# A transformer trunk on one core: the passage into the FFN with its order written out anew

## The chip, the cores and the metric

One core of one Trainium2 chip runs the whole program. The time is device microseconds of one execution. The kernel before: 1216.84, 1217.25 and 1219.11 us, median 1217.25.

## The reference

One layer of a hybrid trunk on 1024 tokens of width 1024: a modulated RMSNorm, one input projection, a Mamba-2 group and a chunked attention group side by side, an output projection, and then the FFN, which is the part that matters here:

```python
h = rmsnorm(x, norm_ffn_w[l]) * (1 + sc_f) + sh_f
x = x + gate_f * conv_ffn(h, w_up, ffn_conv_w, w_down)

def conv_ffn(h, w_up, conv_w, w_down):
    u = causal_dwconv(h @ w_up, conv_w)      # 3 taps, causal
    g, val = jnp.split(u, 2, axis=-1)
    return (jax.nn.silu(g) * val) @ w_down   # 1024 -> 2 x 2816 -> 1024
```

All of it is float32.

## The kernel before

**Engines.** TensorE (PE) multiplies, VectorE (DVE) and ScalarE (ACT) do elementwise work and read the products out of PSUM, GpSimd (POOL) does a little, SyncE (SP) issues loads.

**Float32 by splitting.** Each operand is split into a high and a low half: `split` (L80) lets ScalarE write the rounded high half, and then VectorE the rest, source minus high. `mm3` (L75) makes three matmuls of it: high by high, high by low, low by high. In the third the stationary or moving part is the low half, so a product can begin with the high half of its weights alone.

**Seven products.** The up product h @ w_up is done in the Strassen-Winograd form, seven products of half-size blocks for each of 22 column tiles ("units"). The table `PRODS` (L1070) lists for each product the weight row, the input and the PSUM tile: P1 and P2 go to uX, Q6, Q7 and Q4 to uY, Q5 and P3 to uZ. Each of these adds up in its bank, and after each product `post` (L1103) reads the running value out: P1 to `cv` and P2 to `cg` (ScalarE copies), Q6 to `cg`, Q7 and Q4 to `cv` (VectorE subtractions), P3 to `cg`. Q7 has a second subtraction, of uZ as Q5 left it, before P3 adds onto the same uZ. The subtractions are what frees the bank for the next product that adds to it.

**Units in pairs.** Units i and 11 + i are taken together, eleven pairs. Weight rows come from DRAM into `ya` and `xs` (rows 0 to 3, L1076 and L1077; the next pair is loaded when these rows have been read), `sums` (L1079) makes rows 4 to 7 from them, `prep` (L1086) splits two rows at once into a ring tile `w` of 128x1024 high and as much low, and `prep_s4` (L1242) splits row 7 of both units for P3. The ring of five places (`HOMES`, L1044: places 0 to 2 are buffers of earlier stages, 3 and 4 the buffers r12 and r22 that first hold the raw inputs b12 and b22) gives a place in the order of the two tables FIRST and AGAIN. A place is free when the products with its weights are done, or its first contents have been read.

**Inputs.** The seven inputs b11, b21, t1 to t4 and b22 are made of h once: blocks of h turned by TensorE into `xps`, scaled into the raw buffers (`a`, `rt`, `rb` in the profile), added and subtracted on VectorE, and split: `b11h/b11l`, `b21h/b21l`, `t1h/t1l`, `tH/tL` (t2 and t3 in the first pair of tiles, t4 and b22 in the second). `h_last` (L1218) splits one of the last four, in two halves of 128x1024.

**The passage.** L1193 to L1250 is the stage in which the inputs are finished while the first pair's products already run. Here the engines V, A and T are wrapped in `InOrder` (L45): with `on` set, each instruction is issued behind the one before it in the text. Elsewhere a scheduler with a cost model sets each engine's order. The profile shows rows of the wrapped instructions as L58. Behind the passage the loop (L1328) does what is left of the first pair, then ten more pairs, and the convolution (`conv`, L1127: one ScalarE row `a<-cv`, two VectorE rows), the gate and the stores to DRAM. The last pair's gate is done in the down product, which follows.

## Time and profile before

| | us |
|---|---|
| median of three executions | 1217.25 |
| the profiled execution | 1217.67 |
| its span | 1215.9 |
| TensorE busy | 1162.3 |
| VectorE busy | 942.3 |
| ScalarE busy | 594.9 |

All times within the run are microseconds from the start of the span. The passage begins near 551, the second pair of units at 611.53, the down product after 990. In the rows of the engines a name stands for a tile without its number: `w<-xs` is a weight split of the second unit, `w<-ya` one of the first.

### The profile page before, as it was taken

What the parts mean: (1) busy time and instruction counts of PE and PEld (TensorE: products, weight loads), DVE (VectorE), ACT (ScalarE), POOL (GpSimd) and SP (SyncE); (2) the same over time, 40 slices, a digit from 0 to 9 for tenths busy, and PEclk for the clock granted to TensorE, in tenths of its full rate; (3) what the DMA queues carried; (4) which work ended last, traced back from release to release, by engine and by line L of the source; (5) the groups of instructions that cost most, each with busy time, mean ns of one, the idle gap of its engine ahead of it and who ended that gap; (6) DMA issues with size and microseconds to landing.
All of it is one profiled execution on the core that took longest, in us unless ns stands there. A gap on an engine that the chain in (4) does not pass through costs nothing.

```text
span 1215.9 us, 15656 instructions
## 1 busy us (share of the span) xinstructions
PE 1162.3 (96%) x5802; PEld 976.8 (80%) x5802; DVE 942.3 (77%) x1413; ACT 594.9 (49%) x1001; POOL 195.2 (16%) x174
## 2 busy tenths in 40 slices
PE   5999999999999989999899999999999999999995
PEld 4887888778889978888688888888888888888884
DVE  7756455598697788747899988988889779766976
ACT  4637465663333657676454543444434445433443
POOL 1109373782210134200000000000000000000002
PEclk9999999999999999999999999999999999999998
DMA  9632121323554301141223223322333278733533
GB/s 355 237 94 83 36 74 39 129 81 127 174 174 157 104 18 36 61 147 53 70 80 129 96 104 130 118 81 87 105 130 112 91 265 293 261 118 125 169 117 138
DMA packets 56683, 151.91 MB, mean 125 GB/s; under 512 B 5664, under 2 KB 5792, under 8 KB 55200
## 3 DMA queue, kind: packets, MB, share of 16 engines
q1 hardware_dynamic: 49552, 126.54, 31.3%
q10 hardware_dynamic: 7056, 24.38, 5.0%
q8 instruction: 45, 0.74, 0.3%
q14 instruction: 30, 0.25, 0.1%
HBM read 117.61 MB, written 29.10 MB: 121 GB/s over the span
## 4 chain that ended last, share of the span: by engine, by line
PE 67%; DVE 7%; ACT 2%; DMA 1%; issue 1%; POOL 0%; DVEq 0%; POOLq 0%; SPq 0%; ACTq 0%
PE dn L76 6%; PE dn L77 6%; PE dn L78 6%; PE wops L702 6%; PE uY L76 5%; PE uY L78 5%; PE uY L77 5%; PE uZ L78 3%; PE uZ L77 3%; PE uZ L76 3%; PE uX L78 3%; PE uX L77 3%; PE uX L76 3%; PE s L76 2%; PE s L77 2%; PE s L78 2%
## 5 line engine op out<-in xcount | busy, mean ns | idle before, releaser
L978 POOL TENSOR_TENSOR st<-st,mhalf 128x1 f32<-128x1 f32 x16 | 12.7, 799 | 691.7 <-DVE st L977 680.3
L76 PE MATMUL dn<-w 128*128 128x512 f32 x308 | 111.9, 389 | 0.0
L77 PE MATMUL dn<-w 128*128 128x512 f32 x308 | 111.9, 389 | 0.0
L78 PE MATMUL dn<-w 128*128 128x512 f32 x308 | 103.3, 389 | 0.0
L76 PE MATMUL uY<-tH,w 128*128 128x512 f32 x256 | 99.7, 390 | 1.8 <-ACT w L58 1.8
L410 POOL TENSOR_SCALAR p<-p,st 128x640 f32<-128x640 f32 (+4 forms) x64 | 98.5, 1554 | 13.6 <-DVE st L409 10.4
L78 PE MATMUL uY<-tH,w 128*128 128x512 f32 x256 | 99.6, 389 | 0.0
L77 PE MATMUL uY<-tL,w 128*128 128x512 f32 x256 | 99.6, 389 | 0.0
L85 ACT ACTIVATE w<-ya 128x1024 fp32r<-128x1024 f32 (+1 forms) x41 | 39.1, 955 | 86.1 <-PE uY L78 80.8
L702 PE MATMUL wops<-hH,yhl 128*128 128x512 f32 x224 | 74.9, 403 | 2.6 <-ACT yhl L85 1.4
L78 PEld LDWEIGHTS dn<-w 128*128 128x128 f32 x308 | 57.8, 188 | 12.1
L76 PEld LDWEIGHTS dn<-w 128*128 128x128 f32 x308 | 57.8, 188 | 12.0
L77 PEld LDWEIGHTS dn<-w 128*128 128x128 f32 x308 | 57.8, 188 | 11.9
L85 ACT ACTIVATE pt<-tp 128x512 fp32r<-128x512 f32 (+2 forms) x72 | 36.6, 523 | 48.6 <-PE tp L436 19.7
L404 DVE CUSTOM_DVE_ANT_0 p<-s,bias 128x640 f32<-128x640 f32 (+4 forms) x64 | 40.6, 650 | 25.4 <-PE tp L439 8.5
L86 DVE TENSOR_TENSOR pt<-tp,pt 128x512 fp32r<-128x512 f32 (+2 forms) x72 | 41.9, 595 | 22.3 <-ACT pt L85 13.4
L76 PEld LDWEIGHTS uY<-tH,w 128*128 128x128 f32 x256 | 48.0, 188 | 12.1 <-ACT w L58 2.2
L77 PEld LDWEIGHTS uY<-tL,w 128*128 128x128 f32 x256 | 48.1, 188 | 10.0
L78 PEld LDWEIGHTS uY<-tH,w 128*128 128x128 f32 x256 | 48.1, 188 | 9.9
L85 ACT ACTIVATE w<-xs 128x1024 fp32r<-128x1024 f32 (+1 forms) x41 | 38.9, 952 | 32.4 <-PE uY L78 32.4
L702 PEld LDWEIGHTS wops<-hH,yhl 128*128 128x128 f32 x224 | 42.4, 191 | 11.9 <-ACT yhl L85 1.7
L76 PE MATMUL s<-hH,wh 128*128 128x512 f32 x128 | 50.6, 395 | 0.9 <-DVE ct L515 0.9
(472 smaller groups left out, 3426.8 us busy)
## 6 DMA issues: line engine op xcount, KB each, us to landing
gz<-a ACTq DMA_DIRECT2D x10, 1024.0 KB, 5.3
wos<-in_w_ada_dram SPq DMA_DIRECT2D x18, 512.0 KB, 4.1
ya<-in_w_up_dram SPq DMA_DIRECT2D x11, 768.0 KB, 4.2
xs<-in_w_up_dram SPq DMA_DIRECT2D x11, 768.0 KB, 4.4
adat<-in_w_ada_dram SPq DMA_DIRECT2D x16, 512.0 KB, 6.4
raws<-in_w_ft_dram SPq DMA_DIRECT2D x16, 512.0 KB, 3.6
qk<-in_w_ada_dram SPq DMA_DIRECT2D x14, 512.0 KB, 4.4
gy<-a ACTq DMA_DIRECT2D x10, 512.0 KB, 2.6
```

The source lines that it names most:

```text
L76: T.matmul(ps, lh, rh, start=start, stop=False, skip_group_check=more)
L77: T.matmul(ps, lh, rl, start=False, stop=False, skip_group_check=more)
L78: T.matmul(ps, ll, rh, start=False, stop=stop, skip_group_check=more)
L85: i = A.activation(hi, src, AF.Copy) if ehi is A else ehi.tensor_copy(hi, src)
L86: return i, elo.tensor_tensor(lo, src, f32(hi), ALU.subtract)
L404: V.tensor_tensor_reduce(out=dst, in0=src, in1=bsl, scale=-1.0, scalar=3e38, op0=ALU.add, op1=ALU.min, accum_out=nm)
L410: G.tensor_scalar(pv_, pv_, rr, None, op0=ALU.mult)
L702: i = op(*a, **k)
L978: G.tensor_tensor(r, ms, mhalf[:, 0:1], ALU.pow)
```

## The change

In the passage the text, and so the order on each engine, becomes: the second unit's split for Q5 and Q6 stands ahead of the split of t2 and ahead of the copy of P2 to `cg`. For this `product` gets a switch that leaves the copy out, and `post` is called on its own. The sums for row 6 and the first unit's split for Q7 and Q4 stand ahead of the split of t3, the second unit's behind it. The seventh products (Q7) move from the loop into the passage, the first between the two halves of t4's split, the second behind row 7's sums; the second subtraction of Q7 becomes `minus_z` and ends the passage. The split of the last weights (row 7) is put between the halves of b22's split. The ring gives the seventh tile (these last weights) place 2 instead of 4, and the turn after it runs 0, 4, 1, 3, 2 instead of 2, 0, 1, 3, 4. No arithmetic is added or left out.

```diff
-    FIRST, AGAIN = (0, 1, 2, 0, 1, 3, 4), (2, 0, 1, 3, 4)
+    FIRST, AGAIN = (0, 1, 2, 0, 1, 3, 2), (0, 4, 1, 3, 2)
...
-        def product(self, p):
+        def product(self, p, post=True, z=True):
...
-            self.post(p, ps)
+            if post:
+                self.post(p)
+            if z and p == "Q7":
+                self.minus_z()
...
             elif p == "Q7":
                 V.tensor_tensor(self.v[:, 512:S], ps, self.v[:, 0:512], ALU.subtract)
-                V.tensor_tensor(self.v[:, 512:S], self.v[:, 512:S], self.ps["Z"], ALU.subtract)
...
+        def minus_z(self):
+            V.tensor_tensor(self.v[:, 512:S], self.v[:, 512:S], self.ps["Z"], ALU.subtract)
...
-    h_last("t2", "t2")
-    u0.product("P2")
-    u1.prep("Q5", "Q6")
+    u0.product("P2", post=False)
+    u1.prep("Q5", "Q6")
+    h_last("t2", "t2")
+    u0.post("P2")
     u1.product("P2")
...
     for u in units:
         u.product("Q5")
-    h_last("t3", "b12")
     for u in units:
         u.sums((6,))
-    for u in units:
-        u.prep("Q7", "Q4")
-    for u in units:
-        u.product("Q6")
-    h_last("t4", "b21")
+    u0.prep("Q7", "Q4")
+    h_last("t3", "b12")
+    u0.product("Q6")
+    u1.product("Q6")
+    u1.prep("Q7", "Q4")
+    h_last("t4", "b21", (0,))
+    u0.product("Q7", z=False)
+    h_last("t4", "b21", (1,))
     for u in units:
         u.sums((7,))
-    h_last("b22", "b22")
+    u1.product("Q7", z=False)
+    h_last("b22", "b22", (0,))
     prep_s4(units)
+    h_last("b22", "b22", (1,))
+    for u in units:
+        u.minus_z()
...
-        order = ("Q7", "Q4", "P3") if q == 0 else ("P1", "Q6", "Q5", "Q7", "P2", "Q4", "P3")
+        order = ("Q4", "P3") if q == 0 else ("P1", "Q6", "Q5", "Q7", "P2", "Q4", "P3")
```

First place: ScalarE behind the last piece of t1h, where the second unit's Q5 weights (`w_5466` before, `w_5460` now) are made. Before:

```order
L58 ACTIVATE t1h_4972<-a_4968 128x4x128
L58 ACTIVATE tH0_5444<-rt2_4974 128x1024 x2
L58 ACTIVATE cg_5464<-uX_5382 128x512
L58 ACTIVATE w_5466<-xs_2856 128x1024
L58 ACTIVATE cg_5464<-uX_5400 128x512
```

Now:

```order
L58 ACTIVATE t1h_4972<-a_4968 128x4x128
L58 ACTIVATE w_5460<-xs_2856 128x1024
L58 ACTIVATE tH0_5444<-rt2_4974 128x1024 x2
L58 ACTIVATE cg_5467<-uX_5382 128x512
L58 ACTIVATE cg_5467<-uX_5400 128x512
```

The weights moved ahead of the split of t2 and ahead of the copies into `cg`, whose buffer holds rt (the raw t2) until VectorE has read it.

Second place: VectorE from the reading of Q6 to that of the first Q4. `cv<-uY,cv` is a Q7 subtraction where it comes first for a tile, and Q4's where it comes again. Before:

```order
L58 TENSOR_TENSOR cg_5464<-cv_5413,uY_5538 128x512
L58 TENSOR_TENSOR tL1_5447<-a_4971,tH1_5446 128x1024 x2
L58 TENSOR_TENSOR ya_781<-ya_781 128x512
L58 TENSOR_TENSOR xs_2856<-xs_2856 128x512
L58 TENSOR_TENSOR tL1_5447<-rb22_4976,tH1_5446 128x1024 x2
L1116 TENSOR_TENSOR cv_5395<-uY_5524,cv_5395 128x512
L1116 TENSOR_TENSOR cv_5413<-uY_5538,cv_5413 128x512
L1084 TENSOR_TENSOR ya_781<-ya_781 128x512 x2
L1117 TENSOR_TENSOR cv_5395<-cv_5395,uZ_5486 128x512
L58 TENSOR_TENSOR w_5562<-ya_781,w_5562 128x512
```

Now:

```order
L58 TENSOR_TENSOR cv_5395<-uY_5521,cv_5395 128x512
L58 TENSOR_TENSOR tL1_5447<-a_4971,tH1_5446 128x1024
L58 TENSOR_TENSOR ya_781<-ya_781 128x512
L58 TENSOR_TENSOR xs_2856<-xs_2856 128x512
L58 TENSOR_TENSOR cv_5413<-uY_5535,cv_5413 128x512
L58 TENSOR_TENSOR tL1_5447<-rb22_4976,tH1_5446 128x1024
L58 TENSOR_TENSOR w_5586<-ya_781,w_5586 128x512
L58 TENSOR_TENSOR w_5586<-xs_2856,w_5586 128x512
L58 TENSOR_TENSOR tL1_5447<-rb22_4976,tH1_5446 128x1024
L58 TENSOR_TENSOR cv_5395<-cv_5395,uZ_5486 128x512
L58 TENSOR_TENSOR cv_5413<-cv_5413,uZ_5499 128x512
L1122 TENSOR_TENSOR cv_5395<-uY_5521,cv_5395 128x512
```

The two Q7 subtractions stand ahead of the split of b22 now, and the last weights inside it.

Third place: ScalarE behind the passage, where the second pair's weights are made (`w_5684` and `w_5687` for P1 and Q6, `w_5748` and `w_5751` for Q5 and Q7, `w_5808` for P2 and Q4); this order is the scheduler's. Before:

```order
L58 ACTIVATE w_5562<-xs_2856 128x512
L85 ACTIVATE w_5748<-ya_781 128x1024
L85 ACTIVATE w_5684<-ya_781 128x1024
L1130 ACTIVATE a_5608<-cv_5395,pkt_66 128x1024
L85 ACTIVATE w_5751<-xs_2856 128x1024
L85 ACTIVATE w_5687<-xs_2856 128x1024
L1130 ACTIVATE a_5625<-cv_5413,pkt_66 128x1024
```

Now:

```order
L58 ACTIVATE tH1_5446<-rb22_4976 128x1024
L1136 ACTIVATE a_5608<-cv_5395,pkt_66 128x1024
L85 ACTIVATE w_5748<-ya_781 128x1024
L1136 ACTIVATE a_5625<-cv_5413,pkt_66 128x1024
L85 ACTIVATE w_5751<-xs_2856 128x1024
L85 ACTIVATE w_5684<-ya_781 128x1024
L85 ACTIVATE w_5808<-ya_781 128x1024
```

The convolution's rows `a<-cv` stand ahead of the second pair's weights now, and TensorE's order there (not shown) takes the Q5 products between the first two matmuls of P1 and the rest of it. In the third pair and at the start of the fourth a few products stand elsewhere; behind that the orders are the same.

More of the change, by code (lines that the diff above doesn't have):

```diff
@@ L1100, in product, with post @@
                     start and kt == 0, kt == 3, not start)
-            self.post(p, ps)
-        def post(self, p, ps):
+            if post:
+                self.post(p)
+            if z and p == "Q7":
+                self.minus_z()
+        def post(self, p):
+            ps = self.ps[PRODS[p][2]]
             if p == "P1":
@@ L1216, in tile_block, with h_last @@
     h_pair(1, ("t4", "b22"))
-    def h_last(n, src):
-        for j in range(2):
+    def h_last(n, src, js=range(2)):
+        for j in js:
             h_split(n, src, slice(2 * j, 2 * j + 2))
+    u0.product("P2", post=False)
+    u1.prep("Q5", "Q6")
     h_last("t2", "t2")
-    u0.product("P2")
-    u1.prep("Q5", "Q6")
+    u0.post("P2")
     u1.product("P2")
@@ L1228, in tile_block @@
                                           reuse_waits="tile"))
-    for u in units:
-        u.product("Q5")
-    h_last("t3", "b12")
-    for u in units:
-        u.sums((6,))
-    for u in units:
-        u.prep("Q7", "Q4")
-    for u in units:
-        u.product("Q6")
-    h_last("t4", "b21")
-    for u in units:
-        u.sums((7,))
     def prep_s4(units):
@@ L1246, in prep_s4 @@
             u.w["P3"] = w[:, :, j, :]
-    h_last("b22", "b22")
+    for u in units:
+        u.product("Q5")
+    for u in units:
+        u.sums((6,))
+    u0.prep("Q7", "Q4")
[6 more added lines that the diff above has]
+    h_last("t4", "b21", (1,))
+    for u in units:
+        u.sums((7,))
+    u1.product("Q7", z=False)
+    h_last("b22", "b22", (0,))
     prep_s4(units)
+    h_last("b22", "b22", (1,))
+    for u in units:
+        u.minus_z()
     V.on = A.on = T.on = False
```

## Prediction

> **What bounds the kernel now.** I read the page first, then TensorE's list of waits, then busy time by stretch around the passage, and last each engine's rows there.

> ```profile
> span 1215.9 us, 15656 instructions
> ...
> PE 1162.3 (96%) x5802; PEld 976.8 (80%) x5802; DVE 942.3 (77%) x1413; ACT 594.9 (49%) x1001; POOL 195.2 (16%) x174
> ```

> TensorE (PE) is busy nearly all the time, so only a hole in its row can be won. TensorE's list of waits, for the tiles of the FFN's up product, has three rows:

> ```profile
> PE uY L76 <- ACT w L58: 1.8, 1, 1.8
> ...
> PE uZ L58 <- ACT w L58: 1.6, 1, 1.6
> ...
> PE uZ L58 <- DVE w L58: 0.5, 1, 0.5
> ```

> All three lie in the passage; from the second pair of units on there is none. Busy time by stretch (length, busy time of PE, PEld, DVE, ACT, POOL, then granted clock, DMA share, GB/s):

> ```profile
> 578.15:580.88 2.73, 2.73 (x13) 2.06 (x11) 2.73 (x3) 0.71 (x1) 0.00 (x0) 1.00 0.00 0
> 580.88:583.90 3.02, 0.89 (x3) 0.30 (x2) 1.30 (x2) 2.85 (x4) 0.00 (x0) 0.93 0.01 3
> 583.90:587.45 3.55, 3.54 (x9) 2.83 (x10) 3.39 (x4) 1.47 (x3) 0.00 (x0) 0.58 0.00 0
> 587.45:598.58 11.13, 11.13 (x50) 9.01 (x48) 8.46 (x11) 5.40 (x6) 0.00 (x0) 1.00 0.23 62
> 598.58:600.52 1.94, 0.16 (x1) 0.03 (x1) 1.94 (x4) 0.71 (x2) 0.00 (x0) 1.00 0.90 323
> 600.52:611.53 11.01, 11.01 (x49) 9.09 (x49) 10.76 (x17) 5.72 (x7) 0.00 (x0) 1.00 0.18 72
> 611.53:647.00 35.47, 35.47 (x158) 29.39 (x157) 35.43 (x43) 16.44 (x18) 0.00 (x0) 1.00 0.35 126
> ```

> The reader is to see three things. TensorE stands at 580.88 to 583.90 and at 598.58 to 600.52. After the first stand its granted clock is 0.58 for 3.55 us. And VectorE (DVE) has no slack from 600.52 to 647, although TensorE does not wait there: whoever moves TensorE forward runs into VectorE.

> TensorE's rows at the edges:

> ```profile
> 580.65 0.39 PE L58 MATMUL uZ<-t1h,w 128*128 128x512 f32 x1
> 582.64 0.50 PE L58 MATMUL uZ<-t1h,w 128*128 128x512 f32 x1 [1.61 <-ACT w L58]
> ...
> 583.90 1.22 PE L58 MATMUL uZ<-t1h,w 128*128 128x512 f32 x2 [0.53 <-DVE w L58]
> ...
> 587.67 0.39 PE L58 MATMUL uY<-tH,w 128*128 128x512 f32 x1
> ...
> 600.52 0.47 PE L76 MATMUL uY<-tH,w 128*128 128x512 f32 x1 [1.78 <-ACT w L58]
> ...
> 606.09 0.39 PE L76 MATMUL uZ<-tH,w 128*128 128x512 f32 x1
> ...
> 611.53 0.39 PE L76 MATMUL uX<-b11h,w 128*128 128x512 f32 x1
> ```

> A product is 12 matmuls; the two P3 products fill 606.09 to 611.53, so one takes 2.72 us at full clock.

> **What the removed waits cost.** Second unit's Q5: 580.88 to 587.67 is 6.79 us where 2.72 would do, so 4.07 are lost. Ten of its matmuls ran after 583.90 and would have taken 2.27 at full clock; they took 3.77, so 1.50 of the 4.07 is the clock and 2.57 is waiting. Ahead of the first Q4: 1.94. The rest of the passage is 0.16 over 2.72 a product. Sum 6.17 us. Put differently: nine products remain after 580.88, 9 x 2.72 = 24.48, and without any hole the second pair begins at 605.36 instead of 611.53.

> **Does the change remove both?** ScalarE (ACT) writes the high half of a split, VectorE the low half. Their rows:

> ```profile
> 576.12 0.63 ACT L58 ACTIVATE t1h<-a 128x512 fp32r<-128x512 f32 x1 [1.29 <-DVE a L58]
> 576.85 2.01 ACT L58 ACTIVATE tH<-rt 128x1024 fp32r<-128x1024 f32 x2
> 581.05 0.60 ACT L58 ACTIVATE cg<-uX 128x512 f32<-128x512 f32 x1 [2.19 <-DVE tL L58]
> 581.54 1.05 ACT L58 ACTIVATE w<-xs 128x1024 fp32r<-128x1024 f32 x1
> ...
> 599.81 0.63 ACT L58 ACTIVATE w<-ya 128x512 fp32r<-128x512 f32 x1 [6.96 <-DVE tL L58]
> 600.34 0.61 ACT L58 ACTIVATE w<-xs 128x512 fp32r<-128x512 f32 x1
> ...
> 607.35 1.15 ACT L1130 ACTIVATE a<-cv,pkt 128x1024 f32<-128x1024 f32 x1 [0.74 <-DVE cv L1119]
> ```

> ```profile
> 578.00 0.68 DVE L58 TENSOR_TENSOR a<-a,rt 128x512 f32<-128x512 f32 x1
> 578.61 2.35 DVE L58 TENSOR_TENSOR tL<-rt,tH 128x1024 fp32r<-128x1024 f32 x2
> 582.62 1.23 DVE L58 TENSOR_TENSOR w<-xs,w 128x1024 fp32r<-128x1024 f32 x1 [1.67 <-ACT w L58]
> ...
> 597.42 2.35 DVE L58 TENSOR_TENSOR tL<-rb,tH 128x1024 fp32r<-128x1024 f32 x2
> 599.69 1.28 DVE L1116 TENSOR_TENSOR cv<-uY,cv 128x512 f32<-128x512 f32 x2
> ...
> 611.91 1.28 DVE L1132 SCALAR_TENSOR_TENSOR a<-cv,pkt,a 128x1023 f32<-128x1023 f32 x1
> ```

> From start to next start these are: ScalarE 0.54 for 512 columns (0.49 from PSUM), 0.955 for 1024, 1.06 for the scaled copy of L1130; VectorE 0.60 for 512, 1.14 for 1024, 1.20 for the multiply-add. A result is out after the duration printed (0.68, 1.05, 1.23 and so on). With these I lay out the changed order; times stand on the clock of the run above, which is unaltered up to 576.

> *First hole.* Before, the second unit's weights `w<-xs` stood on ScalarE behind `cg<-uX`, an eviction that needs the buffer of rt and so waits for both tL<-rt. Now they follow t1h: high half 576.66 to 577.71, low half on VectorE behind `a<-a,rt`, 578.61 to 579.84. TensorE wants them at 580.88: 1.0 to spare, the hole closes. What is pushed back: tL<-rt ends at 582.1, wanted by Q6 at 583.60.

> *Second hole.* Before, Q4 of the first unit had to wait for the seventh product's subtraction (599.69), which was queued on VectorE behind two tL<-rb of b22. Now: w of Q7/Q4 high 583.1, low 584.2 to 585.45; tL<-rb of t3 until 587.7, Q7 wants both at 589.04. VectorE stands until the second Q6 is done (589.25); its cg to 589.93, second unit's low half 589.86 to 591.1, wanted at 591.76; half of t4 to 592.2, the first Q7 subtraction 592.1 to 592.8, the other half of t4 to 594.0, wanted by Q4 at 594.48. Second subtraction 595.1 to 595.8, wanted at 597.20. Then b22 and the last weights interleave: 595.7, 596.8, 597.4, 598.05 to 599.3, and the first subtraction of uZ 599.2 to 599.87. P3 adds onto that uZ, so it wants it out at 599.92. Every margin is positive but the last is 0.05: any slip of VectorE there is paid one to one. I take zero here and 0.5 as the upper bound, about one 512-column row.

> The other ring place: the last weights go to place 2, free once the first unit's Q6 has ended (586.3), instead of r22, which is read until the last tL<-rb. That permits the interleaving and costs nothing, since ScalarE reaches them at 594.6. Two posts and two preparations run as before, only elsewhere: no instruction is added.

> **Where the stall goes.** At 605.36 the second pair wants its first weights. VectorE has run since 589.25 without a gap: 600.4 to 601.1 it subtracts the first Q4. ScalarE's first row for the convolution waits for that, and the second pair's weights are queued behind it: a 601.1, w 602.2, a 603.2, w 604.2, and only then w of P1/Q6, 605.15 to 606.2. TensorE waits 0.9 to 1.0. Then it passes Q5 of the first unit, and each low half comes just in time or late: VectorE's rows put the second unit's Q5 low half at 611.7 (0.45 late), the low half of P1 at 614.0 (0.07), one of P2/Q4 at 634.8 (0.31). New waiting: 1.0 + 0.45 + 0.07 + 0.31 = 1.83. VectorE's own account says the same in the large: its idle in the passage before was 1.67 + 0.52 + 2.03 and some 0.5 in smaller pieces, 4.7; now 583.2 to 584.2 and 588.3 to 589.25 remain, 1.9, so it gets ahead by 2.8 only, while TensorE would be ahead by 6.17. It keeps 1.3 us of idle behind the first gapless stretch, at 648:

> ```profile
> 588.14 1.23 DVE L58 TENSOR_TENSOR w<-ya,w 128x1024 fp32r<-128x1024 f32 x1 [0.52 <-ACT w L58]
> ...
> 593.34 0.69 DVE L58 TENSOR_TENSOR cg<-cv,uY 128x512 f32<-128x512 f32 x1 [2.03 <-PE uY L58]
> ...
> 649.35 0.69 DVE L1119 TENSOR_TENSOR cv<-uY,cv 128x512 f32<-128x512 f32 x1 [1.27 <-PE uY L78]
> ```

> So 2.8 + 1.3 = 4.1 is about what VectorE can support, beside 6.17 - 1.83 = 4.34 from the rows. Weights from DRAM are not late: their load is issued at the end of the sums of row 7 (594.6 now, 596.96 before) and took 4.2:

> ```profile
> 596.96 0.33 SPq L1077 DMA_DIRECT2D ya<-in_w_up_dram  x1
> ...
> ya<-in_w_up_dram SPq DMA_DIRECT2D x2, 768.0 KB, 4.2
> ```

> It lands at 598.9, wanted by VectorE at 601. In the third pair and at the start of the fourth a few products stand elsewhere; behind that the engines' rows are in the old order, only shifted, so the rest passes to the end.

> The clock term (1.50) is the soft one: the same length of wait, 1.78, was followed by 1.00 at 600.52. [...]

> **Sum.** Profiled execution: 1217.67 us, 1.77 outside the span. 1217.67 - 4.34 = 1213.3. The median shown is 0.42 below that execution; 1217.25 - 4.34 = 1212.9. I say 1213.0. Its own range, from 0.5 at the narrow place and 1 us on VectorE: 1211.9 to 1214.4.

> **Rivals.**
> - *The whole 6.17 stays* (12%): the waits at the second pair do not come, 1211.1. For it: the scheduler put Q5 ahead so that TensorE has work. Against: ScalarE's queue above leaves 0.9 even if VectorE is 0.1 early.
> - *VectorE starves the second pair longer* (9%): 4 us or more of waits at 605 to 635, or 1.8 with the clock falling there; gain 0 to 2.4, about 1215.8. For it: DVE 35.43 of 35.47. Against: 1.3 us of slack at 649.
> - *The low clock is not of this wait's making* (14%): it comes to other executions at another place or not at all, so only 4.34 - 1.50 = 2.84 is won: 1214.4. For it: the second wait, without a drop.
> - *Slower* (7%): the rotated ring makes a split wait for its place in each later pair; nine pairs at the 0.68 us of one 512-column VectorE row in front of the split are 6.1, net 1217.25 - 4.34 + 6.1 = 1219.0. It decides from 4.34 / 9 = 0.48 us a pair. Against: in both orders a place returns after five splits.

> **How the numbers follow.** Forecast 58%. A measurement of this kernel tells about 0.2% (2.4 us, 1214.8) from no change. Forecast, first rival and two thirds of the third are faster: 0.58 + 0.12 + 0.09 = 0.79, less 0.01 for the spread of the runs (1216.84 to 1219.11): 0.78. The rest of the third and the second rival are the same: 0.14. Slower: 0.07, and 0.01 for the spread: 0.08. The range from the first rival's time to the second's holds some 85%: 1211.0 to 1216.0.

> **What would show it.** In the changed profile: Q5 of both units back to back, no clock below 1.00 near 584; no wait of uY at 598 or a remnant under 0.5 at P3; a new wait of about 1 us of uX on ACT w at the second pair's start (near 606) and one near 611 on DVE w; P3 of the first pair ending at 605 to 606. Wrong would be: waits of uX, uY or uZ after 640, a hole left before Q4 or P3 over 1 us, or a clock of 0.5 at 606.

## The result and the profile after

| | before | changed |
|---|---|---|
| median, 8 executions each | 1217.45 us | 1213.31 us |
| lowest to highest | 1216.45 to 1221.30 | 1212.05 to 1215.50 |
| ratio, 95% interval | | 0.9964, 0.9951 to 0.9977 |
| the profiled execution | 1217.67 | 1213.16 |

The changed kernel is faster by 4.14 us in the median. Its page begins:

```profile
span 1211.4 us, 15654 instructions
...
PE 1160.1 (96%) x5802; PEld 974.6 (80%) x5802; DVE 942.9 (78%) x1413; ACT 594.2 (49%) x1001; POOL 193.9 (16%) x174
```

VectorE's and ScalarE's busy times are what they were (942.9 beside 942.3, 594.2 beside 594.9), so the 4.5 us by which the span is shorter come from work that stands closer and, in TensorE's row (1160.1 beside 1162.3), from less work at half clock. In TensorE's list of waits, for the tiles of the up product, the three rows of before are gone, and one is new:

```profile
PE uX L76 <- ACT w L85: 0.7, 1, 0.7
```

Busy time by stretch around the passage (length, busy time of PE, PEld, DVE, ACT, POOL, then granted clock, DMA share, GB/s), with the same edges as before up to 600.52:

```profile
580.88:583.90 3.02, 3.02 (x15) 2.48 (x14) 2.28 (x3) 1.91 (x3) 0.00 (x0) 1.00 0.07 19
583.90:587.45 3.55, 3.55 (x17) 2.96 (x16) 3.40 (x3) 2.01 (x3) 0.00 (x0) 1.00 0.37 132
587.45:598.58 11.13, 11.13 (x51) 9.22 (x50) 10.19 (x14) 6.03 (x7) 0.00 (x0) 1.00 0.28 85
598.58:600.52 1.94, 1.94 (x9) 1.43 (x9) 1.94 (x4) 0.00 (x0) 0.00 (x0) 1.00 0.79 329
600.52:605.30 4.78, 4.78 (x22) 3.77 (x21) 4.78 (x8) 4.30 (x5) 0.00 (x0) 1.00 0.00 0
605.30:612.00 6.70, 5.93 (x25) 4.44 (x25) 6.70 (x9) 4.99 (x5) 0.00 (x0) 1.00 0.00 0
612.00:647.00 35.00, 35.00 (x155) 28.52 (x154) 34.91 (x43) 14.73 (x17) 0.00 (x0) 1.00 0.35 128
```

The reader sees both holes filled: 3.02 of 3.02 where 0.89 stood, 1.94 of 1.94 where 0.16 stood. The clock behind the first is 1.00 where it was 0.58. What is left open is 0.77 us at 605.30 to 612.00, the start of the second pair. TensorE's rows there (start, duration, engine, line, operation; in brackets the wait and its releaser):

```profile
605.14 0.39 PE L78 MATMUL uZ<-tH,w 128*128 128x512 f32 x1
606.20 0.50 PE L76 MATMUL uX<-b11h,w 128*128 128x512 f32 x1 [0.67 <-ACT w L85]
606.54 0.40 PE L77 MATMUL uX<-b11l,w 128*128 128x512 f32 x1
```

Matmuls of one product start 0.227 apart at full clock. From 605.14 to 606.20 are 1.06, so 0.83 are lost, and the next one follows after 0.34, so another 0.11 is lost right behind the wait. What is waited for stands in ScalarE's rows:

```profile
600.89 1.15 ACT L1136 ACTIVATE a<-cv,pkt 128x1024 f32<-128x1024 f32 x1 [4.29 <-DVE cv L1122]
602.15 1.06 ACT L85 ACTIVATE w<-ya 128x1024 fp32r<-128x1024 f32 x1
603.12 1.14 ACT L1136 ACTIVATE a<-cv,pkt 128x1024 f32<-128x1024 f32 x1
604.16 1.04 ACT L85 ACTIVATE w<-xs 128x1024 fp32r<-128x1024 f32 x1
605.11 1.99 ACT L85 ACTIVATE w<-ya 128x1024 fp32r<-128x1024 f32 x2
```

ScalarE stands idle for 4.29 us, then does a convolution row of the first pair, and only then begins the weights of the second. The weights that TensorE wants at 605.37 are the first half of the 1.99 at 605.11.

**A measure for the experiments.** Whole times of one kernel spread by several microseconds, and the profiles show where that comes from: the first matmul into uX starts anywhere from 565.2 to 570.4 in profiles whose code is the same up to there, as TensorE's clock did or did not fall to half in earlier stages (the profiles record one such stretch of 3.41 us ahead of the passage for the first of these, and 17.07 us in all for the last). So beside each median I give the stretch from that first matmul to the last matmul of the down product. The tile views of before and of the changed kernel give its ends (first and last start are the pair behind the colon's durations):

```profile
L58 PE MATMUL uX<-b11h,w x16: 389/389/397, 566.4 to 571.6; 128*128 128x512 f32 x16
...
L78 PE MATMUL dn<-w x308: 388/389/390, 992.8 to 1201.5; 128*128 128x512 f32 x154
```

```profile
L58 PE MATMUL uX<-b11h,w x16: 389/389/397, 566.2 to 571.5; 128*128 128x512 f32 x16
...
L78 PE MATMUL dn<-w x308: 388/389/389, 988.3 to 1197.1; 128*128 128x512 f32 x154
```

1201.5 - 566.4 = 635.1 before and 1197.1 - 566.2 = 630.9 now. Profiled again, the kernel before gave 635.2 twice and the changed one 630.8 twice, so this measure is good to some 0.1 us where the clock in the stretch is the same. Two single executions below stand far out and are left out of the medians: 1672.34 us with the second pair's weights first and 1467.05 us with the sums on GpSimd, at mean granted clocks of 0.66 and 0.75.

### The profile page after: what moved, and what is told of

Its sections match the earlier page's. It is cut to its first block, busy times and chain, and to the rows that moved or that the text cites. A ratio compares the mean times of both kernels' runs of the same rounds, so it can differ in the third digit from the quotient of the medians.

```text
span 1211.4 us, 15654 instructions
## 1 busy us (share of the span) xinstructions
PE 1160.1 (96%) x5802; PEld 974.6 (80%) x5802; DVE 942.9 (78%) x1413; ACT 594.2 (49%) x1001; POOL 193.9 (16%) x174
## 4 chain that ended last, share of the span: by engine, by line
PE 68%; DVE 7%; ACT 1%; DMA 1%; issue 1%; POOL 0%; DVEq 0%; POOLq 0%; SPq 0%; ACTq 0%
PE dn L76 6%; PE dn L77 6%; PE dn L78 6%; PE wops L702 5%; PE uY L78 4%; PE uY L76 4%; PE uY L77 4%; PE uX L78 3%; PE uX L77 3%; PE uX L76 3%; PE uZ L78 3%; PE uZ L77 3%; PE uZ L76 3%; PE s L76 2%; PE s L77 2%; PE s L78 2%
## 5 line engine op out<-in xcount | busy, mean ns | idle before, releaser
L76 PE MATMUL dn<-w 128*128 128x512 f32 x308 | 111.9, 389 | 0.0
L78 PE MATMUL dn<-w 128*128 128x512 f32 x308 | 103.3, 389 | 0.0
L76 PE MATMUL uY<-tH,w 128*128 128x512 f32 x248 | 96.6, 389 | 0.0
L77 PE MATMUL uY<-tL,w 128*128 128x512 f32 x248 | 96.5, 389 | 0.0
L78 PE MATMUL uY<-tH,w 128*128 128x512 f32 x248 | 96.5, 389 | 0.0
L78 PEld LDWEIGHTS dn<-w 128*128 128x128 f32 x308 | 57.8, 188 | 12.1
L76 PEld LDWEIGHTS dn<-w 128*128 128x128 f32 x308 | 57.8, 188 | 11.9
L76 PEld LDWEIGHTS uY<-tH,w 128*128 128x128 f32 x248 | 46.5, 188 | 10.1 <-DVE cv L1120 0.4
L78 PEld LDWEIGHTS uY<-tH,w 128*128 128x128 f32 x248 | 46.5, 188 | 9.6
L76 PE MATMUL s<-hH,wh 128*128 128x512 f32 x128 | 50.6, 396 | 0.8 <-DVE ct L515 0.8
L1138 DVE SCALAR_TENSOR_TENSOR a<-cv,pkt,a 128x1023 f32<-128x1023 f32 (+1 forms) x40 | 51.1, 1277 | 0.1
## 6 DMA issues: line engine op xcount, KB each, us to landing
ya<-in_w_up_dram SPq DMA_DIRECT2D x11, 768.0 KB, 4.1
xs<-in_w_up_dram SPq DMA_DIRECT2D x11, 768.0 KB, 4.3
```

The source lines that it names most:

```text
L76: T.matmul(ps, lh, rh, start=start, stop=False, skip_group_check=more)
L77: T.matmul(ps, lh, rl, start=False, stop=False, skip_group_check=more)
L78: T.matmul(ps, ll, rh, start=False, stop=stop, skip_group_check=more)
L1138: V.scalar_tensor_tensor(a[:, j:S], c[:, 0:S - j], w[2 - j], a[:, j:S], op0=ALU.mult, op1=ALU.add)
```

## The experiments

All kernels here compute everything. Ratios are taken within runs on one chip; the medians of the kernel before on the three chips were 1217.60, 1217.80 and 1217.91. A ratio is an estimate over all executions and can differ by 0.001 from the quotient of the medians, so the stretch is what the readings below go by.

| kernel | median us | ratio to before, 95% | stretch us |
|---|---|---|---|
| before, profiled twice more | 1220.58, 1216.58 (one execution each) | | 635.2, 635.2 |
| the changed kernel, twice more | 1213.10, 1214.11 | 0.9964 (0.9951 to 0.9977), 0.9967 (0.9956 to 0.9978) | 630.8, 630.8 |
| first hole alone | 1215.20 | 0.9991 (0.9977 to 1.0004) | 633.3 |
| second hole alone | 1217.78 | 1.0000 (0.9989 to 1.0012) | 635.2 |
| changed, old ring | 1214.88 | 0.9983 (0.9971 to 0.9995) | 633.4 |
| changed, first hole made long | 1221.23 | 1.0029 (1.0018 to 1.0040) | 637.5 |
| changed, sums on GpSimd | 1215.78 | 0.9996 (0.9983 to 1.0010) | 634.8 |
| changed, second pair's weights first, three times | 1213.22, 1212.45, 1212.75 | 0.9962 (0.9948 to 0.9976), 0.9959 (0.9945 to 0.9972), 0.9963 (0.9948 to 0.9977) | 629.7, 629.8, 629.8 |

### The changed kernel once more

No edit; it stands beside the next three on one chip.

> The changed kernel unaltered, so that the others of this group stand beside it on one chip. 0.9964 of the kernel before, 1213.3 us; TensorE waits of 0.7 us at 606 and some 0.4 us near 611; no low clock between 576 and 612.

Measured: 1213.10 us, ratio 0.9964, stretch 630.8, one wait of 0.7 of uX, and no low clock in the passage; near 611 some 0.25 us are lost, where 0.4 was expected. The gain and the new wait are properties of the kernel, not of one execution.

### The ring place undone

```diff
-    FIRST, AGAIN = (0, 1, 2, 0, 1, 3, 2), (0, 4, 1, 3, 2)
+    FIRST, AGAIN = (0, 1, 2, 0, 1, 3, 4), (2, 0, 1, 3, 4)
...
     h_last("b22", "b22", (0,))
-    prep_s4(units)
     h_last("b22", "b22", (1,))
+    prep_s4(units)
```

> The changed kernel with the old ring order, so the last weights lie in r22 and their split stands behind the whole split of b22 instead of inside it. Theory: ScalarE cannot write them before VectorE has read r22 to the end (about 599.1), so P3 begins some 2.6 us later than in the changed kernel (near 602.4), and the waits at the second pair shrink in return: net 0.7 to 1.3 us slower than the changed kernel, about 1214.3. Rival (VectorE's supply alone decides, the ring is free): within 0.3 us of the changed kernel.

Measured: 1214.88 us and 633.4, so 2.6 us of the 4.3 are lost again, where 0.7 to 1.3 were expected. TensorE's rows from the last matmul of Q4 to the first of P3, and the stretch behind the wait (columns as above):

```profile
603.69 0.39 PE L78 MATMUL uY<-tH,w 128*128 128x512 f32 x1
606.60 0.50 PE L76 MATMUL uX<-b11h,w 128*128 128x512 f32 x1 [2.52 <-ACT w L85]
...
607.65 0.40 PE L76 MATMUL uZ<-tH,w 128*128 128x512 f32 x1
```

```profile
608.00:611.50 3.50, 3.50 (x10) 2.72 (x9) 3.50 (x5) 2.10 (x2) 0.00 (x0) 0.51 0.00 0
```

The wait bears the name uX because four matmuls of the second pair now stand ahead of P3 in TensorE's order. Its place is straight behind Q4, in front of the first pair's P3. Counted from the first matmul into uX, P3 begins 37.26 us on, where it began 33.56 us on in the changed kernel: 3.70 later (2.6 expected). ScalarE's and VectorE's rows show what P3 lacks, its weights and the subtractions of uZ:

```profile
602.04 0.63 ACT L58 ACTIVATE w<-ya 128x512 fp32r<-128x512 f32 x1 [5.45 <-DVE tL L58]
```

```profile
605.98 1.28 DVE L58 TENSOR_TENSOR cv<-cv,uZ 128x512 f32<-128x512 f32 x2
```

The wait alone accounts for 1.8 more than in the changed kernel, and behind it the clock is at 0.51: ten matmuls in the stretch that holds fifteen at 0.227. The low clock is what the expectation had left out; the smaller waits near 611 and 634 do not come in return. The size of each is not split off here. The ring place, which the prediction costed at nothing, is therefore a necessary part of the change together with the order that it permits: with the old place the last weights can't be made between the halves of b22, and P3 comes late. The new place with the old order of the two splits was not run.

### The first hole alone

The kernel before, with the second unit's weights ahead of t2 and P2 read out later:

```diff
-    h_last("t2", "t2")
-    u0.product("P2")
-    u1.prep("Q5", "Q6")
+    u0.product("P2", post=False)
+    u1.prep("Q5", "Q6")
+    h_last("t2", "t2")
+    u0.post("P2")
```

> The kernel before with only the first part of the change: the second unit's Q5 weights ahead of the split of t2, the copy of P2 to cg later; old ring, Q7 behind the passage. From the first uX matmul to the last matmul of the down product the kernel before took 635.1 us in its profile, the changed one 630.9. Theory (one chain of VectorE behind both holes): the first hole closes, but TensorE only arrives earlier at work that VectorE has not done; about 2.4 us of waiting ahead of the first Q7 and 1.5 ahead of the first Q4, in sum the old length but for the clock: 633.2 without a low clock, 634.7 with one, so 0.4 to 1.9 us faster than before. Rival (each hole its own price): 4.1 us faster, 631.0.

Measured: 1215.20 us and 633.3, a gain of 1.8 in the stretch (in whole time the ratio's interval includes 1). The first hole cost 4.07 us, and only 1.8 of it came back. TensorE's rows show two waits that were not there before:

```profile
590.85 0.47 PE L76 MATMUL uY<-tH,w 128*128 128x512 f32 x1 [2.22 <-DVE cg L58]
...
597.79 0.47 PE L76 MATMUL uY<-tH,w 128*128 128x512 f32 x1 [1.23 <-ACT w L58]
```

And VectorE's rows ahead of the first:

```profile
588.89 1.22 DVE L58 TENSOR_TENSOR w<-xs,w 128x1024 fp32r<-128x1024 f32 x1
590.02 1.28 DVE L58 TENSOR_TENSOR cg<-cv,uY 128x512 f32<-128x512 f32 x2
```

TensorE arrives earlier at Q7 and finds the reading of Q6 (`cg<-cv,uY`) queued behind two weight splits on VectorE. The two pieces of idle time in the first hole, 1.61 and 0.53, have become 2.22 ahead of Q7, with 1.23 in front of Q4 instead of 1.78. (The profile puts the wait before Q4 down to ScalarE's weights. VectorE's subtraction for Q7 ends 0.15 us ahead of Q4, as `cg<-cv,uY` does ahead of Q7, and in the kernel with the old ring Q4 starts before those weights are made.) The clock stays at 1.00 throughout: what is won is the low clock, and for the rest some 0.3 to 0.5 of waiting.

### The second hole alone

The changed kernel with the first part taken back:

```diff
-    u0.product("P2", post=False)
-    u1.prep("Q5", "Q6")
     h_last("t2", "t2")
-    u0.post("P2")
+    u0.product("P2")
+    u1.prep("Q5", "Q6")
```

> The changed kernel with only the first part undone: the split of t2 and the copy of P2 stand ahead of the second unit's Q5 weights again; new ring, Q7 inside, last weights inside the split of b22. Theory: the hole at 580.9 to 583.9 is back with its low clock, the one before Q4 is gone, and the waits at the second pair stay as in the changed kernel, since VectorE comes as much later as TensorE: first uX to last matmul about 635.0, no gain over the kernel before (0.1 us). Rival (each hole its own price): 1.9 us faster than before, 633.2.

Measured: 1217.78 us, ratio 1.0000, stretch 635.2: no gain at all. TensorE's rows:

```profile
582.35 0.50 PE L58 MATMUL uZ<-t1h,w 128*128 128x512 f32 x1 [1.64 <-ACT w L58]
...
583.61 1.20 PE L58 MATMUL uZ<-t1h,w 128*128 128x512 f32 x2 [0.52 <-DVE w L58]
...
610.37 0.50 PE L76 MATMUL uX<-b11h,w 128*128 128x512 f32 x1 [0.67 <-ACT w L85]
```

The first hole is there as before, the second is closed, and the second pair waits. So the two parts are worth 1.8 and -0.1 alone and 4.3 together. The holes are not two independent losses: whichever is closed alone hands most or all of its waiting to the next place. That VectorE's chain is what stands behind all of these places is read from its rows, not tested by itself.

### The first hole made long

Six copies of the first half of t2's high part (the same values written again) on ScalarE in front of the weights, to see what a longer stand does to the clock:

```diff
     u0.product("P2", post=False)
+    for _ in range(6):
+        A.activation(hb_["t2"][0][:, 0:2, :], hr["t2"][:, 0:2, :], AF.Copy)
     u1.prep("Q5", "Q6")
```

> The changed kernel with six extra copies on ScalarE (0.96 us each, they write the first half of t2's high part early, which is written again in its place) ahead of the second unit's Q5 weights. TensorE waits some 3.6 us and 0.8 us there instead of not at all. Theory (the low clock follows a hole of 2 us or more, for one stretch of about 3.4 us): one low stretch that costs 1.5 to 1.7 us, first uX to last matmul 630.9 + 5.0 + 1.6 = 637.5. Rival A (the lost clock grows with the hole): two low stretches, 639. Rival B (the hole has nothing to do with the clock): clock 1.00, 635.9.

Measured: 1221.23 us and 637.5, the number expected, though not in the parts expected. Busy time by stretch:

```profile
582.45:585.97 3.52, 0.18 (x2) 0.00 (x1) 0.02 (x1) 3.46 (x5) 0.00 (x0) 0.88 0.00 0
585.97:591.95 5.98, 5.94 (x13) 4.26 (x14) 5.09 (x6) 4.32 (x6) 0.00 (x0) 0.50 0.11 32
```

The hole is 3.34 us by TensorE's waits, and the clock is at half for 6.8 us, twice as long as in any other profile of the passage; some of it falls into the hole itself. Thirteen matmuls take 5.94 us where 2.95 would do. So about 3.5 us are the hole's and some 3.0 are lost behind it, most of that to the clock (matmuls 0.427 apart) and the rest to three first gaps of 0.59 to 0.67. A half clock behind this wait is thus made by it, as the forecast took it. The number was right only because two errors cancelled: the hole was shorter than expected, and the low clock lasted the two stretches that rival A had named.

### The sums on GpSimd

If VectorE's work is what the second pair waits for, eight of its rows can go to GpSimd, which is idle here:

```diff
-                V.tensor_tensor(b[:, o, :], b[:, i0, :], b[:, i1, :], ALU.add)
+                (G if self.i % KH == 1 else V).tensor_tensor(b[:, o, :], b[:, i0, :], b[:, i1, :], ALU.add)
```

> The changed kernel with the eight sums of the second pair's weight rows (0.60 us each on VectorE, 4.8 us together) made on GpSimd, which is idle there (1.36 us for 128x512 in an earlier stage, so 10.9 us in all). Theory (VectorE's backlog is what eats 1.8 of the 6.2 us): every wait of uX, uY and uZ goes; 1.2 to 1.9 us faster than the changed kernel, about 1211.6. Rival: the two engines slow each other down where both work in SBUF, VectorE's 0.60 us rows grow by 10 % or more while GpSimd adds, and the gain is under 0.5 us or negative.

Measured: 1215.78 us and 634.8: nearly the whole gain is gone, as the rival had it. TensorE waits 3.05 us at 614 for a low half on VectorE, and the clock falls behind it (0.58 from 615 to 619):

```profile
614.18 0.50 PE L78 MATMUL uX<-b11h,w 128*128 128x512 f32 x1 [3.05 <-DVE w L86]
```

Rows of GpSimd and VectorE:

```profile
608.56 2.28 POOL L1084 TENSOR_TENSOR ya<-ya 128x512 f32<-128x512 f32 x1
```

```profile
611.85 2.28 DVE L86 TENSOR_TENSOR w<-ya,w 128x1024 fp32r<-128x1024 f32 x1
614.04 0.68 DVE L1127 TENSOR_TENSOR cg<-cg,uZ 128x512 f32<-128x512 f32 x1
```

Both engines are slower here. The split's low half takes 2.28 where it takes 1.22 in the kernel before, GpSimd's addition takes 2.28 where its first three took 1.27 each, and VectorE is later than without the help. The last section has more on it.

### The second pair's weights first

The remaining wait comes from ScalarE's queue. This kernel keeps the first pair's last convolution, gate and store back until the second pair's first two weight splits are issued:

```diff
-                self.conv(1, self.v)
+                if self.i % KH:
+                    self.conv(1, self.v)
...
+            if q == 1 and n == 0:
+                with tc.issue_after(last_split[0].ins), tc.issue_after(last_split[1].ins):
+                    for u in held:
+                        u.conv(1, u.v)
+                for u in held:
+                    u.finish()
+                store_pair(held)
...
-        if q < KH - 1:
+        if q == 0:
+            held = units
+        elif q < KH - 1:
```

> The changed kernel with the first pair's convolution on cv held back until the second pair's first weights (P1 and Q6, both halves, both units) have been issued; nothing else is altered. Theory (ScalarE's queue order makes the wait at 606): the wait there shrinks from 0.7-1.0 to about 0.3 us, the one near 611 goes, 0.3 us comes up near 622; 0.8 to 1.2 us faster than the changed kernel, about 1212.3. Rival (VectorE's supply sets it whatever the order): within 0.3 us of the changed kernel, the waits only elsewhere.

Measured: 1213.22 us, ratio 0.9962, stretch 629.7. In the list of waits no row of uX, uY or uZ is left. Since the median didn't show what the stretch did, it ran twice more, on other chips, the second time beside the changed kernel.

> The kernel with the second pair's first weights ahead of the first pair's convolution once more, for its time: from the first uX matmul to the last matmul of the down product 629.7 us in its first profile against 630.9 and 630.8 of the changed kernel. Theory: 629.7 again, TensorE without a wait of uX, uY or uZ; in time 1.1 us under the changed kernel, 0.9954 of the kernel before, if the stages ahead of the passage run alike. Rival: the span comes out at 630.8 and the first profile was a chance.

> The kernel with the second pair's first weights ahead of the first pair's convolution a third time. Theory: 629.7 us from the first uX matmul to the last matmul, and 1.1 us under the changed kernel in the median, about 1212.2. Rival: the gain in that stretch does not show in the time, because the stages ahead of it vary by more: medians within 0.5 us.

> The changed kernel a third time, to stand beside the next one on one chip: about 1213.3 us, first uX matmul to last matmul 630.8.

Measured: 1212.45 and 1212.75 us; the changed kernel beside the latter 1214.11. Busy time by stretch of the second run:

```profile
580.88:605.00 24.12, 24.12 (x108) 19.74 (x106) 22.25 (x30) 12.21 (x15) 0.00 (x0) 1.00 0.25 88
605.00:612.00 7.00, 6.95 (x31) 5.45 (x30) 7.00 (x9) 6.89 (x7) 0.00 (x0) 1.00 0.09 26
612.00:647.00 35.00, 35.00 (x155) 28.73 (x154) 35.00 (x42) 14.72 (x17) 0.00 (x0) 1.00 0.34 123
```

TensorE's open time at the second pair's start is 0.05 us, where the changed kernel had 0.77; by the starts of its matmuls some 0.3 us are still lost there, about what was expected. The stretch is 1.1 us shorter in each of three profiles. In whole time the median over all executions is 1213.0 for this kernel (23) and 1213.6 for the changed one (25): the same direction, but too small to be told apart. It is the best of the versions by the stretch, and clearly faster than the kernel before.

### The kernel before, profiled twice more

For the question whether the half clock follows the first wait by chance, two more profiles of the kernel before:

> The kernel before once more with a profile, to see the granted clock at its two holes again. Theory (the first hole brings the low clock nearly always, since most of it lies close together): 0.50 for 3.4 us from about 583 on, 635.1 us from the first uX matmul to the last matmul. Rival (it depends on where the hole falls against a period of 3.4 us, and the second hole may bring it instead): another pattern, 633.6 without any low stretch, 636.6 with two.

> The same as the run before it, one more draw: 0.50 for 3.4 us from about 583 on and 635.1 us by the theory, another pattern (633.6 without a low stretch, 636.6 with two) by the rival.

Measured: in both the waits of the passage are 1.6, 0.5 and 1.8, as in the first profile, and in both the clock falls behind the first stand and stays at 1.00 behind the second. The stretch that shows it in one of them:

```profile
586.00:590.00 4.00, 3.48 (x10) 2.56 (x9) 3.79 (x5) 1.92 (x4) 0.00 (x0) 0.57 0.01 2
```

With the kernel that has the second hole closed alone, that makes four profiles out of four with the first hole open.

## Why the prediction was right

**Sign, size and the two holes.** Forecast 1213.0 for the median, measured 1213.31; forecast 4.34 off, measured 4.33 from the first matmul into uX to the last into uZ (425.72 before, from 566.38 to 992.10; 421.39 now, from 566.24 to 987.63). Q5 of both units is back to back, and Q4 is no longer waited for. Each of the margins laid out row by row held, and with them the weights from DRAM.

**The narrow place.** Zero was taken for the 0.05 us before P3, with 0.5 as the bound. TensorE's rows there:

```profile
599.54 0.39 PE L78 MATMUL uY<-tH,w 128*128 128x512 f32 x1
599.80 0.47 PE L76 MATMUL uZ<-tH,w 128*128 128x512 f32 x1
600.11 0.40 PE L77 MATMUL uZ<-tL,w 128*128 128x512 f32 x1
```

0.26 and 0.31 instead of 0.227 twice: 0.11 lost, and no wait that the profile names.

**The new waits** are the term that was a little too large: 1.83 forecast, about 1.6 measured. The first, 0.9 to 1.0, is 0.83 and has the cause given: the convolution row stands ahead of the weights on ScalarE; the kernel that moves it removes the wait. The one near 611 is 0.26 and not 0.45, and it ends with VectorE's low half as said. The one at 614 is not there. The one at 634 is 0.14 and not 0.31, and of another kind: it ends with VectorE's subtraction for Q7, not with a low half. In their place comes what the prediction didn't have: after each wait the next matmul starts 0.34 behind the first instead of 0.23, 0.11 lost three times.

**The clock term.** The 1.50 us were taken from ten matmuls between 583.90 and 587.67. One gap in them, the first, is 0.59, where its neighbours at half clock are 0.427 apart. So about 0.17 of the term is that first gap, and the clock alone cost about 1.3. The sum isn't touched by this, since both went with the hole.

**VectorE's account** (2.8 us ahead and 1.3 of slack, together 4.1) said nearly the same as the sum of the rows, and its slack was used as said. The idle time at the end of its gapless stretch was 1.27 in the kernel before (ahead of its row at 649.35) and is now 0.29:

```profile
648.51 0.69 DVE L1127 TENSOR_TENSOR cg<-cg,uZ 128x512 f32<-128x512 f32 x1 [0.29 <-PE uZ L78]
```

The three runs with the weights first got 1.1 more, and there VectorE is busy 35.00 of 35.00 from 612 to 647. How much more could be won in front of the second pair with VectorE this full was not tested.

**The rivals.** That the whole 6.17 stays is excluded by the wait at 606. That VectorE starves the second pair longer is excluded for this change, but the sums on GpSimd went there, with a wait of 3.05 and the clock falling. (The old ring's 2.52 stands ahead of the first pair's P3.) That the ring costs a wait in every pair is excluded: no wait is named after 606, and without the new place the kernel is slower. That the low clock isn't of the first wait's making falls by the four profiles of four, by the changed kernel's 1.00 and by the lengthened hole. The 2.84 that would then have been won stands against the measured 4.33.

**What the prediction had by luck.** It took the two holes as terms of a sum. They are not: 1.8 and -0.1 alone, 4.3 together. The sum came out because the change closes both at once and because VectorE was laid out through the whole passage, not because each hole is worth its length. That 4.33 falls within 0.01 of 4.34 is luck as well: the new waits came out smaller than forecast, and the gaps of 0.34 behind them and the 0.11 at the narrow place made up for it.

## What to carry to other kernels

A hole's length is what closing it wins only if the engine behind it has time in hand: lay that engine's rows out through to the next place that needs it, and close the holes that share it together. Behind a stand of the matmul engine look at the granted clock: here some 1.3 us of the 4.3 was work done at half rate. A buffer's place in a ring can cost no instruction and still be what permits an order; and where whole runs spread, compare a stretch between two marks that all kernels have.

## What the runs showed of the hardware

```profile
580.05:583.46 3.41, 1.72 (x7) 0.78 (x5) 1.74 (x2) 2.41 (x4) 0.00 (x0) 1.00 0.00 0
597.11:600.52 3.41, 1.63 (x8) 1.04 (x7) 3.41 (x5) 0.71 (x2) 0.00 (x0) 1.00 0.78 229
```

Then of the changed kernel with the old ring, up to the fall of the clock at 608.10,

```profile
604.69:608.10 3.41, 1.50 (x6) 1.24 (x7) 3.41 (x7) 3.13 (x4) 0.00 (x0) 1.00 0.00 0
```

and of the lengthened hole, up to the fall at 585.16 and on from there:

```profile
581.75:585.16 3.41, 0.88 (x4) 0.38 (x2) 0.00 (x0) 3.35 (x4) 0.00 (x0) 1.00 0.00 0
585.16:588.57 3.41, 2.56 (x5) 1.66 (x6) 2.62 (x3) 2.65 (x3) 0.00 (x0) 0.50 0.00 0
```

The half clock follows the first, the third and the fourth of these rows, not the second; the fifth is at half clock itself, and 3.42 us more at 0.50 follow it. Busy time doesn't part them (1.72 is followed by it, 1.63 is not). Four to seven matmuls run in the rows at full clock that it follows, eight in the one that it doesn't; but ahead of 443.52, where the matmuls have other shapes, eight run as well (1.38 us busy), and it follows. Nor does the length of a wait part them: behind 1.61 and 0.53 us in the first hole the clock was 0.50, behind 1.78 in the second it was 1.00, and behind 2.22 in the kernel with the first hole alone it was 1.00 too. A rule for when the clock falls was not shown.

**VectorE and GpSimd at the same time.** In the kernel before, a split's low half takes VectorE 1.22 us and its multiply-add 1.28. With the sums on GpSimd, GpSimd's first three additions took 1.27 each:

```profile
600.31 3.81 POOL L1084 TENSOR_TENSOR ya<-ya 128x512 f32<-128x512 f32 x3 [28.41 <-DMA ya<-in_w_up_dram]
```

Its other five, beside VectorE's splits and multiply-adds, took 4.55 for two, 2.28 for one and 4.47 for two. Of the VectorE rows beside them three took 2.28 to 2.33 and one, a split's low half at 614.64, 1.71; the fifth, a multiply-add at 607.98, was followed by the next after 1.63. VectorE's row with one operand in PSUM (`cg<-cg,uZ`, at 607.38 and 614.04) kept its 0.68. So the price here is 0.5 to 1.1 us for a row that is held up; what makes it so was not shown.
